# Reading compression windows straight from split keys with a stride, x's squares from a row-major copy, and other first pieces in a fused decoder layer

## The chip, the core and the metric

One core of a Trainium2 chip runs the whole layer in one launch. The metric is device microseconds from launch to end on that core, median of the runs shown. An execution's time is a little longer than the span of its profile, which goes from the first to the last instruction.

## What is computed

One decoder layer on 256 tokens of width 2048, all in float32: a token mixer (gMLP gating, dilated attention, native sparse attention), cross attention, and a squared-ReLU MLP of width 8192. What the change touches is the first normalization and the compressed keys and values:

```
def rms_norm(x, g):
    y = xf * lax.rsqrt(jnp.mean(xf * xf, axis=-1, keepdims=True) + EPS)
...
def compress_blocks(kraw, pos, w1, w2):      # blocks of 32 keys, stride 16 -> 15 blocks
    sub = kraw.reshape(bsz, ng, S // CMP_STRIDE, CMP_STRIDE, hd)
    blocks = jnp.concatenate([sub[:, :, :-1], sub[:, :, 1:]], axis=3) + pos
    h = jax.nn.gelu(blocks.reshape(bsz, ng, n_c, CMP_LEN * hd) @ w1)
    return h @ w2
```

`compress_blocks` runs for the keys and for the values, on 2 groups each; `w1` is 4096 x 128.

## The kernel before, in words

Every large product is made in a split form: a float32 operand is taken apart into a rounded part (`wh`, `hi`) and the remainder (`wl`, `lo`), and the product is hi·hi + hi·lo + lo·hi. ScalarE makes the rounded part by a copy (L82), VectorE the remainder by a subtraction (L83). A block of weights is 128 x 1024 numbers (512 KB). It is loaded by SyncE's queue into one of five `raw` buffers (`load_raw`, L78), split into one of three `wh` and three `wl` buffers, and used by TensorE.

`gemm_t` (L179) makes a transposed product: for each of the 4 blocks and each of 4 slices of 128 rows, `products_t` issues two matmuls with 512 moving columns (`mains`, L164: `wh` against the activation's hi and lo parts side by side) and two with 256 (`lows`, L169: `wl` against hi). `gemm` (L198) makes an untransposed product of 24 matmuls a block (L212). Matmuls here are named after their accumulator: `cmp`, `k`, `sg`, `wv`, `ph`, and so on.

The program begins with `cmp` (L240 to L265), the raw keys (m = 0) and values (m = 1) of the compressed branch. It loads x transposed (`xres`) and both weights in pieces, interleaved, in the steps `((1, 1, 2), (2, 2), (4,), (4,))` of 128-row slices for the four blocks b. Each piece of x is scaled and split into `hx` (`put_act`, L87 on ScalarE, L88 on VectorE), each piece of weights into `wh` and `wl`, and the products of a slice can start when its pieces are split. Then come `k0` (first keys of the other branches), `k1`, `sg` and `wv`. While `k0` runs, the generator `squares` adds up the squares of x: eight ScalarE squares (L101) and seven VectorE sums (L103) of 128 x 512, one sum on GpSimd (L115), two matmuls against a column of ones (`pss`, L117); from it come the reciprocal norm `rx` (L123) and its copy along the free dimension, `rxb` (two matmuls `psb`, L133).

While `k1` and `sg` run, the generator `compress` (L324) makes the compressed keys, then the values. VectorE gathers the 15 windows of 32 keys into `win` and adds the position (L330, which reads with a step of 16 numbers); the windows are split into `blk`, which lies as 32 slices of 60 columns (30 hi, 30 lo). For each of 32 positions l, two matmuls with 128 moving columns follow: `blk[:, l, :M2]` (30 stationary columns) with `wl` (L341), `blk[:, l, :]` (60) with `wh` (L343). They accumulate in `ph`; a copy `hh`, a product with a selection matrix `sel` (`pj`), a Gelu (`hg`, `hr`) and the second weight (`pk`, `pv`) end it. Gelu and the gates' Exp (L382) need different activation tables; a load of a table is an ACT instruction.

The order on each engine is set by a scheduler that works through the program with modelled costs; each engine and each queue then runs its list in order. Squares, `compress` and the gates so lie between the splits of weights on ScalarE and VectorE.

Of the kernel before, what the change touches and what calls it, by code (L numbers as in the profile page):

```python
# [37 lines left out]
def trunk_kernel(ctx: ExitStack, tc: tile.TileContext, a, out):  # L38
# [257 lines left out]
    rx = rstd(mean_eps(ssq, "mx"), "rx")
# [14 lines left out]
    for m in range(2):  # L311
# [9 lines left out]

    blk = slot("hC", "blk").rearrange("p k a s -> p (k a s)")[:, :LCMP * 2 * M2].rearrange("p (l m) -> p l m", l=LCMP)

    def compress():  # L324
        for m, which in enumerate(("k", "v")):
            win = cw[:, 4 * S:4 * S + LCMP * M2].rearrange("p (l g n) -> p l g n", l=LCMP, g=2)
# [426 lines left out]
def _masks(np):  # L753
# [4 lines left out]
    for window, d in ((128, 1), (512, 4), (2048, 16)):  # L758
        count += (dist >= 0) & (dist <= window) & (dist % d == 0)
    mb = np.where(count > 0, np.log(np.maximum(count, 1)), NEG).astype(np.float32)  # L760
    ends = np.arange(NCMP) * 16 + 31
# [20 lines left out]
def _arrays(np, i):  # L782
# [12 lines left out]
    def c1(w):  # L795
# [46 lines left out]
```

## Time and profile before

| | |
|---|---|
| median of 3 runs | 1195.46 us (1195.13 to 1196.47) |
| profiled execution | 1195.4 us |
| its span | 1193.6 us |
| TensorE matmuls busy | 1177.7 us, 99% |
| VectorE / ScalarE busy | 740.6 us / 589.2 us |
| chain that ended last | PE 97%, VectorE 1%, issue 1%, ScalarE 1% |
| DMA | 224 MB, mean 188 GB/s |

The table is read from the chain: where TensorE has 97% of it, only what makes TensorE wait or gives it more to do moves the end. "Busy" of a matmul includes a modelled end, so TensorE can be paced by something else for part of its busy time; starts of successive instructions tell more than durations. A load of stationary columns (PEld) runs beside the matmul before it.

### The profile page before, as it was taken

To read this page: it belongs to the slowest core of one execution; us is meant where nothing else is said; L and a number is where in the kernel's file an instruction comes from. 1 tells how busy PE (TensorE), PEld (TensorE's weight loads), DVE (VectorE), ACT (ScalarE), POOL (GpSimd) and SP (SyncE) were. 2 spreads that over 40 slices of the span, in tenths; PEclk is the share of its full clock that TensorE was granted. 3 is DMA by queue.
4 is the path that set the end of the run, shared out by engine and by line. 5 is a ranking of instruction groups with operands and counts; after the bars stand their busy time and mean duration, and the time that the engine had idled before them with its cause. 6 is when DMAs were issued, how large, how long until landed. Compare 5 with 4: busy or idle time off the path is not lost.

```text
span 1193.6 us, 16484 instructions
## 1 busy us (share of the span) xinstructions
PE 1177.7 (99%) x6450; PEld 1016.2 (85%) x6450; DVE 740.6 (62%) x939; ACT 589.2 (49%) x811; POOL 13.0 (1%) x18
## 2 busy tenths in 40 slices
PE   8999999999999999999999999999999999999996
PEld 6898888888888889888888888888888888888885
DVE  7875876569776567665545565545566445656554
ACT  7564555466544467544433444433444333444443
POOL 1000000000000000000000000000000000000000
PEclk9999999999999999999999999999999999999998
DMA  8776444556555554555555556665655655556653
GB/s 294 228 258 187 130 124 141 179 182 225 185 192 192 180 198 139 178 190 193 194 193 194 185 187 193 194 193 189 190 188 182 205 193 195 179 193 191 193 181 106
DMA packets 65673, 224.24 MB, mean 188 GB/s; under 512 B 7995, under 2 KB 9531, under 8 KB 65467
## 3 DMA queue, kind: packets, MB, share of 16 engines
q1 hardware_dynamic: 65307, 222.14, 57.9%
q8 instruction: 50, 0.82, 0.3%
q10 hardware_dynamic: 288, 1.05, 0.3%
q14 instruction: 28, 0.23, 0.1%
HBM read 221.06 MB, written 2.10 MB: 187 GB/s over the span
## 4 chain that ended last, share of the span: by engine, by line
PE 97%; DVE 1%; issue 1%; ACT 1%; DMA 0%; SPq 0%; POOLq 0%; POOL 0%; DVEq 0%; ACTq 0%
PE dn L212 28%; PE up L164 20%; PE up L169 10%; PE wo L164 5%; PE cq L164 3%; PE wo L169 2%; PE xo L153 2%; PE v L212 2%; PE bv L212 2%; PE mv L212 2%; PE k L164 1%; PE cq L169 1%; PE bq L164 1%; PE xq L164 1%; PE u L164 1%; PE mk L164 1%
## 5 line engine op out<-in xcount | busy, mean ns | idle before, releaser
L83 DVE TENSOR_TENSOR wl<-raw,wh 128x1024 fp32r<-128x1024 f32 (+3 forms) x412 | 493.2, 1200 | 325.7 <-ACT wh L82 324.6
L82 ACT ACTIVATE wh<-raw 128x1024 fp32r<-128x1024 f32 (+3 forms) x412 | 426.5, 1038 | 428.3 <-PE dn L212 185.5
L164 PE MATMUL up<-h,wh 128*128 128x512 f32 x1024 | 316.9, 395 | 0.0
L212 PE MATMUL dn<-wh,hid 128*128 128x512 f32 x992 | 306.1, 389 | 0.0
L169 PEld LDWEIGHTS up<-h,wl 128*128 128x128 f32 x1024 | 187.6, 188 | 42.2
L212 PEld LDWEIGHTS dn<-wh,hid 128*128 128x128 f32 x992 | 186.2, 188 | 38.7
L169 PE MATMUL up<-h,wl 128*128 128x256 f32 x1024 | 197.0, 279 | 0.0
L212 PE MATMUL dn<-wl,hid 128*128 128x512 f32 x496 | 193.2, 390 | 1.1 <-DVE wl L83 1.1
L164 PEld LDWEIGHTS up<-h,wh 128*128 128x128 f32 x1024 | 158.4, 189 | 2.7
L212 PEld LDWEIGHTS dn<-wl,hid 128*128 128x128 f32 x496 | 93.1, 188 | 21.4 <-DVE wl L83 2.0
L164 PE MATMUL wo<-mix,wh 128*128 128x512 f32 x256 | 79.1, 395 | 0.0
L169 PEld LDWEIGHTS wo<-mix,wl 128*128 128x128 f32 x256 | 46.5, 188 | 10.3
L193 ACT ACTIVATE half<-up 128x512 f32<-128x512 f32 x32 | 19.2, 599 | 63.6 <-PE up L164 63.6
L195 DVE TENSOR_TENSOR half<-up,half 128x512 f32<-128x512 f32 x32 | 22.2, 693 | 43.5 <-ACT half L193 43.5
L169 PE MATMUL wo<-mix,wl 128*128 128x256 f32 x256 | 49.0, 279 | 0.0
L164 PE MATMUL cq<-hx,wh 128*128 128x512 f32 x128 | 40.4, 396 | 0.0
L164 PEld LDWEIGHTS wo<-mix,wh 128*128 128x128 f32 x256 | 39.7, 189 | 0.8
L672 DVE SCALAR_TENSOR_TENSOR xt<-dn,m,xt 128x512 f32<-128x512 f32 (+1 forms) x34 | 22.9, 715 | 14.4 <-PE dn L212 14.4
L82 ACT ACTIVATE hid<-half 128x512 fp32r<-128x512 f32 x32 | 20.2, 632 | 16.6 <-DVE half L723 16.6
L169 PEld LDWEIGHTS cq<-hx,wl 128*128 128x128 f32 x128 | 23.5, 188 | 5.1
L164 PE MATMUL cmp<-hx,wh 128*128 128x512 f32 x64 | 21.3, 432 | 5.3 <-ACT wh L82 5.2
L169 PE MATMUL cq<-hx,wl 128*128 128x256 f32 x128 | 25.7, 280 | 0.0
(286 smaller groups left out, 1279.3 us busy)
## 6 DMA issues: line engine op xcount, KB each, us to landing
raw<-in_w_up SPq DMA_DIRECT2D x128, 512.0 KB, 4.4
raw<-in_w_down SPq DMA_DIRECT2D x128, 512.0 KB, 4.4
raw<-in_w_t SPq DMA_DIRECT2D x52, 512.0 KB, 3.8
raw<-in_w_out SPq DMA_DIRECT2D x32, 512.0 KB, 4.0
raw<-in_w_bv SPq DMA_DIRECT2D x8, 512.0 KB, 3.7
raw<-in_w_v SPq DMA_DIRECT2D x8, 512.0 KB, 3.6
raw<-in_w_mk SPq DMA_DIRECT2D x8, 512.0 KB, 4.1
raw<-in_w_q SPq DMA_DIRECT2D x8, 512.0 KB, 4.4
```

The lines of the kernel that those rows point to most:

```text
L82: nc.scalar.activation(hi, src, AF.Copy)
L83: nc.vector.tensor_tensor(lo, src, f32(hi), op=ALU.subtract)
L153: nc.tensor.matmul(acc[:, f, 0, :], w[:, kk, fs], x[:, kk, l, :], start=(kk == 0 and j == 0), stop=(kk == 3 and j == 2))
L164: nc.tensor.matmul(acc[:, f].rearrange("p a s -> p (a s)"), wh[:, kk, f * P:(f + 1) * P], xk, start=start, stop=stop)
L169: nc.tensor.matmul(acc[:, f, 0, :], wl[:, kk, f * P:(f + 1) * P], x[:, kk, 0, :], start=False, stop=False)
L193: nc.scalar.activation(lo, acc[:, :, 1, :], AF.Copy)
L195: nc.vector.tensor_tensor(d, acc[:, :, 0, :], lo, op=ALU.add)
L212: nc.tensor.matmul(acc[t][:, :n], lhs[k // 4][:, k % 4, l, ts], w[:, kk, :], start=(k == 0 and j == 0), stop=(k == KD - 1 and j == 2))
L672: nc.vector.scalar_tensor_tensor(xs, acc[t][:, cs], r3[:, t:t + 1], xs, op0=ALU.mult, op1=ALU.add)
```

## The change

It has four parts.

- **Windows.** `win` and `blk` are gone. The scaled keys are split as they lie, into `kps[m]` (hi and lo; for each, two groups of 256 positions and a third group that holds the 32 position vectors and zeros). The stationary operand for position l is a strided view: 96 columns, every 16th number from l on (48 for the `wl` product), 64 bytes apart. A group gives 16 columns: for the keys 15 windows and one that doesn't exist, for the positions one vector and zeros. `sel` (96 x 30) adds the position's row and drops the rest.
- **Squares of x.** x is loaded a second time with tokens on partitions (two loads of 1 MB), and four ScalarE squares of 128 x 1024 with an accumulated sum replace L101, L103, L115 and `pss`.
- **First pieces.** The steps become `((1, 3), (4,), (4,), (4,))`. The gains `gT` are loaded from ScalarE's queue.
- **First matmuls.** Eight float32 matmuls of 128 x 128 on a constant tile (`pw`) are issued ahead of all others.

The diff, cut:

```diff
+M3 = 3 * S // 16
...
+    nc.scalar.dma_start(gT, a["gT"])
...
+    wm = cp.tile([P, P], F32, name="wm")
+    nc.gpsimd.memset(wm, 1.0)
+    pw = pmisc.tile([P, P], F32, tag="sc", name="pw")
+    for _ in range(8):
+        nc.tensor.matmul(pw, wm, wm, start=True, stop=True)
...
-        for step in ((1, 1, 2), (2, 2), (4,), (4,))[b]:
+        for step in ((1, 3), (4,), (4,), (4,))[b]:
...
-                    if k == 0:
-                        nc.sync.dma_start(gT, a["gT"])
...
+    xs = [slot("hB", f"x{t}", F32).rearrange("p k a s -> p (k a s)") for t in range(2)]
+    for t in range(2):
+        with tc.issue_after(loads[-1].ins):
+            nc.sync.dma_start(xs[t], a["x"][t * P:(t + 1) * P, :])
...
+    kpf = [slot("hC", f"kp{m}").rearrange("p k a s -> p (k a s)")[:, :6 * S + 16] for m in range(2)]
+    kps = [t[:, :6 * S].rearrange("p (a g s) -> p a g s", a=2, g=3) for t in kpf]
...
-        for b in range(4):
-            for n in (2 * b, 2 * b + 1):
-                add_squares(ssq, xres[:, 2 * n:2 * n + 2, :], n == 0)
+        for t in range(2):
             yield
+            for i in range(2):
+                xi = xs[t][:, i * 1024:(i + 1) * 1024]
+                nc.scalar.activation(xi, xi, AF.Square, accum_out=ssqx[:, t, i:i + 1])
...
-    rx = rstd(mean_eps(ssq, "mx"), "rx")
+    nc.vector.tensor_reduce(mx, ssqx, axis=AX.X, op=ALU.add)
+    nc.vector.tensor_scalar(mx, mx, 1.0 / D, EPS, op0=ALU.mult, op1=ALU.add)
+    rx = rstd(mx, "rx")
...
+        split(kp[:, 0, :2, :], kp[:, 1, :2, :], km)
...
-            for g in range(2):
-                kr = kraw[:, 2 * m + g, :]
-                src = bass.AP(tensor=kr.tensor, offset=kr.offset, ap=[kr.ap[0], [1, LCMP], [16, NCMP]])
-                nc.vector.tensor_tensor(win[:, :, g, :], src,
-                                        C["posT"][:, :, None].to_broadcast([P, LCMP, NCMP]), op=ALU.add)
-            split(blk[:, :, :M2], blk[:, :, M2:], win.rearrange("p l g n -> p l (g n)"))
...
+                    blk = kpf[m][:, l:l + 16 * 2 * M3 - 15:16]
...
-                    nc.tensor.matmul(ph[:M2], blk[:, l, :M2], wl[:, i, :], start=False, stop=False)
+                    nc.tensor.matmul(ph[:M3], blk[:, :M3], wl[:, i, :], start=False, stop=False)
                     if l > 0:
-                        nc.tensor.matmul(ph, blk[:, l, :], wh[:, i, :], start=False, stop=(l == LCMP - 1))
+                        nc.tensor.matmul(ph, blk, wh[:, i, :], start=False, stop=(l == LCMP - 1))
```

How it moves the order. SyncE's queue at the program's start; the queue before (`xres` is x, `raw` the weights):

```order
L254 DMA xres<-in_xT 128x256
L257 DMA gT<-in_gT 128x64
L258 DMA raw<-in_w_t 128x256 x2
L254 DMA xres<-in_xT 128x256
L258 DMA raw<-in_w_t 128x256 x2
L254 DMA xres<-in_xT 128x512
L258 DMA raw<-in_w_t 128x512 x2
L254 DMA xres<-in_xT 128x512
L258 DMA raw<-in_w_t 128x512 x2
```

and with the change:

```order
L263 DMA xres<-in_xT 128x256
L265 DMA raw<-in_w_t 128x256 x2
L263 DMA xres<-in_xT 128x768
L265 DMA raw<-in_w_t 128x768 x2
L263 DMA xres<-in_xT 128x1024
L265 DMA raw<-in_w_t 128x1024 x2
L263 DMA xres<-in_xT 128x1024
L265 DMA raw<-in_w_t 128x1024
L263 DMA xres<-in_xT 128x1024
L265 DMA raw<-in_w_t 128x1024 x3
L286 DMA x_317<-in_x 128x2048
L286 DMA x_318<-in_x 128x2048
```

The second slice of x now comes with the third and fourth, and the two loads of x by rows stand behind the last `cmp` weights and the first weights of `k0`.

TensorE inside `compress`, a few of the 128 matmuls of `ph` (size: stationary by moving columns); before, with the buffers' numbers:

```order
L341 MATMUL ph_521<-wl_525,blk_493 30x128
L343 MATMUL ph_521<-wh_524,blk_493 60x128
```

and with the change:

```order
L354 MATMUL ph<-wl,kp_332 48x128
L356 MATMUL ph<-wh,kp_332 96x128
```

Their number and place stay; the stationary operand grows from 30 and 60 to 48 and 96 columns, and is now the strided view.

ScalarE between `sg` and `wv`, where the Gelu of the compressed values (`hr`) meets the Exp of the gates; before:

```order
L82 ACTIVATE wh<-raw 128x1024 x2
L365 ACTIVATE hr<-pj 128x15 x2
L381 ACTIVATE vs<-sg,rx 128x256
L382 ACT_TABLE_LOAD
L382 ACTIVATE gate<-sg,nrx 128x24
L381 ACTIVATE vs<-sg,rx 128x256
L382 ACTIVATE gate<-sg,nrx 128x24
L82 ACTIVATE wh<-raw 128x1024 x4
```

and with the change:

```order
L91 ACTIVATE wh<-raw 128x1024 x2
L398 ACTIVATE vs<-sg,rx 128x256
L399 ACT_TABLE_LOAD
L399 ACTIVATE gate<-sg,nrx 128x24
L398 ACTIVATE vs<-sg,rx 128x256
L378 ACT_TABLE_LOAD
L378 ACTIVATE hr<-pj 128x15 x2
L399 ACT_TABLE_LOAD
L399 ACTIVATE gate<-sg,nrx 128x24
L91 ACTIVATE wh<-raw 128x1024 x4
```

`hr` moves between the two gates, which takes two more loads of tables; on TensorE `pj`, from which `hr` is made, moves from the middle of the last blocks of `sg` to behind them. The `wh` behind it all are those of the third and fourth block of `wv` and of the two blocks after it.

## Rows read from the trace of the kernel before

**Rows 1.** The page: span, TensorE's busy time, shares of the chain that ended last.

```profile
span 1193.6 us, 16484 instructions
...
PE 1177.7 (99%) x6450; PEld 1016.2 (85%) x6450; DVE 740.6 (62%) x939; ACT 589.2 (49%) x811; POOL 13.0 (1%) x18
...
PE 97%; DVE 1%; issue 1%; ACT 1%; DMA 0%; SPq 0%; POOLq 0%; POOL 0%; DVEq 0%; ACTq 0%
```

**Rows 2.** Windows of the first 25 us: the stretch and its length, busy time of each engine (and instructions), granted clock, mean DMA share, GB/s.

```profile
0.00:5.00 5.00, 0.46 (x1) 0.47 (x2) 1.25 (x6) 2.78 (x5) 0.80 (x7) 1.00 0.48 142
5.00:10.00 5.00, 5.00 (x16) 3.95 (x15) 2.52 (x7) 3.18 (x8) 0.00 (x0) 1.00 0.91 260
10.00:15.00 5.00, 4.56 (x25) 3.84 (x25) 5.00 (x10) 5.00 (x11) 0.00 (x0) 1.00 1.00 369
15.00:20.00 5.00, 4.85 (x27) 3.79 (x26) 4.89 (x11) 5.00 (x10) 0.00 (x0) 1.00 1.03 414
20.00:25.00 5.00, 4.61 (x25) 3.69 (x25) 5.00 (x8) 4.78 (x9) 0.00 (x0) 1.00 1.03 345
```

**Rows 3.** Timeline of TensorE from the first matmul to the start of `k0`: start, time, line, product, shapes, count, idle time before it and its releaser.

```profile
4.54 2.07 PE L164 MATMUL cmp<-hx,wh 128*128 128x512 f32 x4 [4.54 <-ACT wh L82]
...
8.97 1.05 PE L169 MATMUL cmp<-hx,wl 128*128 128x256 f32 x4
10.46 1.25 PE L164 MATMUL cmp<-hx,wh 128*128 128x512 f32 x4 [0.44 <-ACT wh L82]
...
22.23 0.63 PE L164 MATMUL cmp<-hx,wh 128*128 128x512 f32 x2
...
22.92 0.63 PE L164 MATMUL cmp<-hx,wh 128*128 128x512 f32 x2
...
29.22 0.50 PE L117 MATMUL pss<-ones,ssq 128*128 128x1 f32 x4
29.58 0.48 PE L169 MATMUL cmp<-hx,wl 128*128 128x256 f32 x2
...
31.99 0.61 PE L164 MATMUL k<-hx,wh 128*128 128x512 f32 x2
```

**Rows 4.** Groups of instructions in the first 90 us, forms apart: line, engine, operation, out<-in, shapes, count; busy us, mean ns of one; idle time before them.

```profile
L83 DVE TENSOR_TENSOR wl<-raw,wh 128x1024 fp32r<-128x1024 f32 x26 | 31.5, 1223 | 8.0 <-ACT wh L82 7.9
L82 ACT ACTIVATE wh<-raw 128x1024 fp32r<-128x1024 f32 x27 | 28.1, 1056 | 12.1 <-PE k L164 4.8 <-PE wv L212 3.5 <-PE sg L212 1.6
...
L87 ACT ACTIVATE hx<-xres,gT 128x256 fp32r<-128x256 f32 x16 | 7.1, 498 | 2.9 <-DMA xres<-in_xT 2.0 <-DMA gT<-in_gT 0.9
...
L103 DVE TENSOR_TENSOR ssq<-ssq,sq 128x512 f32<-128x512 f32 x7 | 4.8, 688 | 0.1
L101 ACT ACTIVATE sq<-xres 128x512 f32<-128x512 f32 x7 | 4.1, 616 | 0.0
...
L382 ACT ACT_TABLE_LOAD x1 | 1.3, 1283 | 0.0
```

**Rows 5.** The instructions of `ph` (shortest, median and longest ns, first and last start), and of `psc`, a later product with 128 stationary and 30 moving columns.

```profile
L341 PEld LDWEIGHTS ph<-wl,blk x64: 105/107/112, 46.4 to 73.1; 128*30 128x30 f32 x64
...
L343 PEld LDWEIGHTS ph<-wh,blk x62: 130/132/135, 46.5 to 73.2; 128*60 128x60 f32 x62
...
L447 PEld LDWEIGHTS psc<-kcT,q x32: 187/192/192, 105.7 to 152.4; 128*128 128x128 f32 x32
```

**Rows 6.** Timeline of TensorE: successive matmuls of `ph`, and 16 of `psc`.

```profile
47.08 0.22 PE L341 MATMUL ph<-wl,blk 128*30 128x128 f32 x1
47.14 0.22 PE L343 MATMUL ph<-wh,blk 128*60 128x128 f32 x1
47.20 0.22 PE L341 MATMUL ph<-wl,blk 128*30 128x128 f32 x1
...
150.73 1.94 PE L447 MATMUL psc<-kcT,q 128*128 128x30 f32 x16
```

**Rows 7.** VectorE's readers of the raw keys (the gather with a step of 16 numbers, the scaling without one), and a later operation on rows of 15 numbers that lie together.

```profile
L330 DVE TENSOR_TENSOR cw<-cw,posT x4: 996/1003/1010, 38.2 to 44.3; 128x480 f32<-128x480 f32 x4
...
L313 DVE TENSOR_TENSOR cw<-cw,rxb x2: 683/684/686, 37.0 to 37.6; 128x512 f32<-128x512 f32 x2
...
L459 DVE TENSOR_TENSOR scm<-scm,cm x2: 284/284/284, 123.6 to 155.1; 128x120 f32<-128x120 f32 x2
```

**Rows 8.** Timeline of ScalarE, VectorE and TensorE between `sg` and `wv`, each engine by itself.

```profile
77.08 0.48 ACT L381 ACTIVATE vs<-sg,rx 128x256 f32<-128x256 f32 x1 [0.61 <-PE sg L212]
77.56 1.28 ACT L382 ACT_TABLE_LOAD   x1
78.86 0.28 ACT L382 ACTIVATE gate<-sg,nrx 128x24 f32<-128x24 f32 x1
79.04 0.47 ACT L381 ACTIVATE vs<-sg,rx 128x256 f32<-128x256 f32 x1
...
79.56 2.02 ACT L82 ACTIVATE wh<-raw 128x1024 fp32r<-128x1024 f32 x2
...
80.65 1.23 DVE L83 TENSOR_TENSOR wl<-raw,wh 128x1024 fp32r<-128x1024 f32 x1
...
76.82 0.28 PE L212 MATMUL wv<-wh,hx 128*128 128x256 f32 x1
76.94 0.28 PE L212 MATMUL wv<-wl,hx 128*128 128x256 f32 x1
```

More of the change, by code (lines that the diff above doesn't have):

```diff
@@ L273, in consts @@
                 nc.sync.dma_start(C[name], a[name].partition_broadcast(P) if name == "bs" else a[name])
-    consts([("ident", [P, P]), ("posT", [P, LCMP]), ("sel", [2 * M2, M2]), ("hmask", [P, 4]), ("rowv", [P, 2])])
+    xs = [slot("hB", f"x{t}", F32).rearrange("p k a s -> p (k a s)") for t in range(2)]
+    for t in range(2):
+        with tc.issue_after(loads[-1].ins):
+            nc.sync.dma_start(xs[t], a["x"][t * P:(t + 1) * P, :])
+    consts([("ident", [P, P]), ("posT", [P, LCMP]), ("sel", [2 * M3, M2]), ("hmask", [P, 4]), ("rowv", [P, 2])])
     ident = C["ident"]
-    cw = slot("hC", "cw", F32).rearrange("p k a s -> p (k a s)")
-    kraw = cw[:, :4 * S].rearrange("p (g s) -> p g s", g=4)
+    kraw = slot("hB", "kraw", F32).rearrange("p k a s -> p (k a) s")
+    kpf = [slot("hC", f"kp{m}").rearrange("p k a s -> p (k a s)")[:, :6 * S + 16] for m in range(2)]
+    kps = [t[:, :6 * S].rearrange("p (a g s) -> p a g s", a=2, g=3) for t in kpf]
     vs = slot("hC", "vs", F32).rearrange("p k a s -> p (k a s)")
@@ L283, in trunk_kernel @@
     kcat = slot("hB", "kcat").rearrange("p (g a) b s -> p g a b s", g=2)
-    ssq = sp.tile([P, 2, S], F32, tag="ssq", name="ssq")
+    ssqx = cp.tile([P, 2, 2], F32, name="ssqx")
     def squares():
@@ L289, in squares @@
             join(acc, "cmp", kraw[:, 2 * m:2 * m + 2, :])
-        for b in range(4):
-            for n in (2 * b, 2 * b + 1):
-                add_squares(ssq, xres[:, 2 * n:2 * n + 2, :], n == 0)
+        for t in range(2):
             yield
+            for i in range(2):
+                xi = xs[t][:, i * 1024:(i + 1) * 1024]
+                nc.scalar.activation(xi, xi, AF.Square, accum_out=ssqx[:, t, i:i + 1])
+        yield
     acc_k0 = gemm_t(hx, a["w_t"][KV], "k0", between=squares())
-    rx = rstd(mean_eps(ssq, "mx"), "rx")
+    mx = cp.tile([P, 2], F32, name="mx")
+    nc.vector.tensor_reduce(mx, ssqx, axis=AX.X, op=ALU.add)
+    nc.vector.tensor_scalar(mx, mx, 1.0 / D, EPS, op0=ALU.mult, op1=ALU.add)
+    rx = rstd(mx, "rx")
     rxb = along_free(rx, "rxb")
@@ L309, in join_split @@
         split(hi, lo, j)
-    for m in range(2):
+    for m, kp in enumerate(kps):
         km = kraw[:, 2 * m:2 * m + 2, :]
         nc.vector.tensor_tensor(km, km, rxb[:, None, :].to_broadcast([P, 2, S]), op=ALU.mult)
+        split(kp[:, 0, :2, :], kp[:, 1, :2, :], km)
     join_split(acc_k0, kcat[:, :, 0, 0, :], kcat[:, :, 1, 0, :], "k0", rxb)
@@ L320, in trunk_kernel @@
     vcz = cp.tile([P, 2, 4, HD], F32, name="vcz")
-    blk = slot("hC", "blk").rearrange("p k a s -> p (k a s)")[:, :LCMP * 2 * M2].rearrange("p (l m) -> p l m", l=LCMP)
     def compress():
         for m, which in enumerate(("k", "v")):
-            win = cw[:, 4 * S:4 * S + LCMP * M2].rearrange("p (l g n) -> p l g n", l=LCMP, g=2)
-            for g in range(2):
-                kr = kraw[:, 2 * m + g, :]
-                src = bass.AP(tensor=kr.tensor, offset=kr.offset, ap=[kr.ap[0], [1, LCMP], [16, NCMP]])
-                nc.vector.tensor_tensor(win[:, :, g, :], src,
-                                        C["posT"][:, :, None].to_broadcast([P, LCMP, NCMP]), op=ALU.add)
-            split(blk[:, :, :M2], blk[:, :, M2:], win.rearrange("p l g n -> p l (g n)"))
-            ph = pmisc.tile([2 * M2, P], F32, tag="sc", name="ph")
+            ph = pmisc.tile([2 * M3, P], F32, tag="sc", name="ph")
             for b in range(4):
@@ L338, in compress @@
                     l = 8 * b + i
+                    blk = kpf[m][:, l:l + 16 * 2 * M3 - 15:16]
                     if l == 0:
-                        nc.tensor.matmul(ph, blk[:, l, :], wh[:, i, :], start=True, stop=False)
-                    nc.tensor.matmul(ph[:M2], blk[:, l, :M2], wl[:, i, :], start=False, stop=False)
+                        nc.tensor.matmul(ph, blk, wh[:, i, :], start=True, stop=False)
+                    nc.tensor.matmul(ph[:M3], blk[:, :M3], wl[:, i, :], start=False, stop=False)
                     if l > 0:
-                        nc.tensor.matmul(ph, blk[:, l, :], wh[:, i, :], start=False, stop=(l == LCMP - 1))
+                        nc.tensor.matmul(ph, blk, wh[:, i, :], start=False, stop=(l == LCMP - 1))
                 yield
@@ L347, in compress @@
                 nc.sync.dma_start(w2, a[f"c{which}2"])
-            hh = sp.tile([2 * M2, P], F32, tag="hh", bufs=1, name="hh")
+            hh = sp.tile([2 * M3, P], F32, tag="hh", bufs=1, name="hh")
             nc.scalar.activation(hh, ph, AF.Copy)
@@ L371, in compress @@
             yield
+    for kf, kp in zip(kpf, kps):
+        nc.gpsimd.memset(f32(kp[:, 0, 2, LCMP:]), 0.0)
+        nc.gpsimd.memset(f32(kf[:, 5 * S + LCMP:]), 0.0)
+        split(kp[:, 0, 2, :LCMP], kp[:, 1, 2, :LCMP], C["posT"])
     cgen = compress()
@@ L760, in _masks @@
     mb = np.where(count > 0, np.log(np.maximum(count, 1)), NEG).astype(np.float32)
+    sel = np.zeros((3, 16, 2, NCMP), np.float32)
+    for g in range(2):
+        sel[g, :NCMP, g] = np.eye(NCMP)
+    sel[2, 0] = 1
     ends = np.arange(NCMP) * 16 + 31
@@ L770, in _masks @@
         "triu": np.triu(np.ones((P, P), np.float32)),
-        "sel": np.concatenate([np.eye(M2), np.eye(M2)]).astype(np.float32),
+        "sel": np.tile(sel.reshape(M3, M2), (2, 1)),
         "hmask": np.repeat(np.eye(4), 32, axis=0).astype(np.float32),
@@ L802, in _arrays @@
     d = {
-        "xT": actT(f["x"][0]), "memT": actT(f["mem"][0]),
+        "x": f["x"][0], "xT": actT(f["x"][0]), "memT": actT(f["mem"][0]),
         "gT": np.stack([gains(f[n][0]) for n in ("norm_mix", "norm_xattn", "norm_mem", "norm_mlp")], axis=1),
```

## The prediction, written before the change ran

> **What bounds the kernel now.** I read the chain of waits first: TensorE has 97% of it, and its matmuls are busy for 1177.7 of 1193.6 us [rows 1]. So a term counts only where TensorE waits or gets more to do; freed ScalarE and VectorE time counts nothing by itself. Then the windows and the timeline of the head, the stretch where TensorE does wait. The 32 groups of `cmp`, each two matmuls of 512 and two of 256 columns, take 0.69 us each when nothing holds them (22.23 to 22.92) [rows 3]: 22.1 us in all. They begin at 4.54 and `k0` begins at 31.99 [rows 3], 27.45 us; 5.3 us are lost. The first four groups account for 2.7 of it: they fill 4.54 to 10.02 (8.97 + 1.05), 5.48 us instead of 2.76 [rows 3]. Four matmuls of 256 columns in 1.05 us, less the tail of the last, start some 213 ns apart, which is the 1.2 GHz level of the clock; at 22.23 they run at 2.4 GHz. (The granted clock reads 1.00 there [rows 2], against the rows; I go by the starts.) `pss` takes 0.36 (29.22 to 29.58) [rows 3]. The rest, some 2 us, is waiting for splits, at 10.02 to 10.46 and where blocks of 1024 columns first arrive. From 10 to 25 us ScalarE and VectorE have no free time, and the DMA engines neither [rows 2]. Behind `k0` TensorE has no gap that a faster neighbour could close.
>
> **Head.** The squares leave ScalarE's and VectorE's queues of the head: 8 x 0.616 = 4.9 us and 7 x 0.688 = 4.8 us [rows 4]. What then ends last is the transfers. By the windows 0.71 MB have come by 5 us, 2.01 by 10, 3.86 by 15, 5.93 by 20 [rows 2]. Block 0 is now the first slices (0.39 MB), then x (0.39), weights (0.39), weights (0.39): 1.57 MB, in by 5 + 0.86/0.260 = 8.3 us. A copy of 768 columns takes some 0.85 us (between 0.616 for 512 and 1.056 for 1024 [rows 4]), so the second `wh` stands at 9.15. TensorE's list wants it after one pair of matmuls; the rest of block 0 (six groups, 4.15 us, less that pair's 0.45) ends at 12.9. Block 1: x in at 10.25, four copies of 0.44 (0.498 with pipeline ends [rows 4]) to 12.0, `wh` to 13.05, `wl` to 14.25: the first low products wait 0.8 us, and block 1 ends near 19.5. Blocks 2 and 3 are then paced by TensorE: 16 x 0.69 = 11.0, `k0` at 30.5, a gain of 1.5. Where larger pieces let the transfers run from 4 us at the 414 GB/s that the stretch from 15 us has [rows 2], weights of block 0 stand 1.7 us earlier, the wait in block 1 shrinks, and the gain is 3.8. These are the ends; I take **-2.0**, nearer the first, since the measured rate of that stretch is the nearer row. In it the missing `pss` is 0.36. The eight `pw` matmuls start near 1.1 us, when TensorE could do nothing else until 4.1; two passes each at up to 213 ns make 3.4 us, to 4.5: they take no time from `cmp`. If TensorE leaves 1.2 GHz as long after its first work as before (10.02 - 4.54), it is at 6.6 us instead of 10; slices two to four then run fast, but they start at 9.15 anyway, so this is worth little beyond the 1.5.
>
> **Second load of x.** 2.1 MB behind 6.3 + 0.5 MB: 8.9 MB are in by 20 + 2.97/0.414 = 27.2 us [rows 2]. Two squares of 1024 (as the copy, 1.056 [rows 4]) end at 29.4, sums, power and diagonal near 32; `psb` stands behind the first matmuls of `k0`'s second block, 30 + 2.8 + 0.45 = 33.2. Covered by 1 us; without that cover, each us of delay is one of TensorE. The split of the scaled keys, 2 x 0.68 and two copies, ends some 6 us before the first `ph`. Both at nothing. `gT`, now on ScalarE's queue, frees SyncE 0.4 us earlier; the first matmul waits for `pw`.
>
> **Compressed products.** 128 matmuls with 128 moving columns, now 60 ns apart: a pair takes 0.12 us (47.08 to 47.20) [rows 6]. The load of 30, 60 and 128 contiguous stationary columns takes 107, 132 and 192 ns [rows 5]; where matmuls are short, loads of 128 set the pace, (1.94 - 0.26)/15 = 0.112 us each [rows 6], 0.875 ns a column. So 60 columns (0.053) hide under a matmul today. 96 contiguous columns would be 0.084, 48 still hidden: a pair of 0.144, and 64 pairs cost 64 x 0.024 = 1.5 us. That is the lower end; less is excluded, since neither the number of matmuls nor their columns fall.
>
> But the columns now lie 64 bytes apart, and no load in the trace reads so. The nearest row is VectorE's gather, with the same step over the same keys: 480 numbers in 1003 ns, where 512 contiguous take 684 [rows 7]. At 1.05 ns a number (1223 for 1024 against 684 for 512 [rows 4, 7]) 480 would take 650; the step adds 353/480 = 0.74 ns to each. That it is the step and not the short runs of 15 follows from the 120 numbers in runs of 15 in 284 ns [rows 7], no more than the contiguous price. With 0.74 added a column of a load costs 1.61 ns: 96 take 0.155, 48 take 0.077, neither hidden, a pair 0.232, and the term is 64 x 0.112 = 7.2 us. At the gather's full 1.79 ns a number it is 0.172 + 0.086, 8.8 us: the upper end. I take **+7.2**.
>
> The Trainium skill's page "SBUF — State Buffer", in the section "Specifications (TRN2)", says that memory lines are 16 bytes long and that full bandwidth needs at least two hits on a line, every crossing being penalised. The gather agrees, with 1.79 ns against 1.05; the page gives no price, and no run here shows one for a stationary load.
>
> **Tables.** Two more loads of 1.283 us [rows 4] stand between `sg` and the third block of `wv`. From the end of `sg`, on the clock of [rows 8] with `pj` moved behind it: `vs` at 76.75, table, gate, `vs` to 79.15, table to 80.43, two `hr` to 80.67, table to 81.95, gate, and the third `wh` to 83.2 instead of 80.6. VectorE does `hr`'s copy by 81.0, after the gate three small operations, then the third `wl` at 83.25 to 84.45. TensorE starts `wv` at 76.82 and does 24 matmuls of 0.12 us a block [rows 8]; it reaches `pv` after seven of block 2, at 80.5, and waits 0.4 for `hr`; 0.36 later it goes on, and reaches the second matmul of the third block at 83.5, where `wl` is 0.95 late. **+1.35**; ends 0 (the chain ahead starts earlier by what ScalarE has been freed of) and 2.6 (both loads).
>
> Removed work of `win` and `blk`, four gathers and two splits, lay beside TensorE and is worth nothing. GpSimd's memsets are done before anyone waits.
>
> **Sum.** The profiled execution took 1195.4 us (0.06 under the median). -2.0 + 7.2 + 1.35 = +6.55: **1202.0 us**. By its parts' ends, 1199 to 1204.5. A measurement of this kernel can tell about 0.2%, 2.4 us, from no change.
>
> **Rivals.**
> A. *The strided load costs no more than a contiguous one.* Loads and matmuls read through different paths than VectorE, and a load runs at half a matmul's column rate, so it may have room. Then -2.0 + 1.5 + 1.35 = +0.85: 1196.3, no change (1195 to 1198). For it: a load is slow already (0.875 ns, where a moving column takes 0.69/1536 = 0.45 [rows 3]). Against it: the gather. The Trainium skill's page "TensorE: Matmul & The Clock Gate", section "LDWEIGHTS", makes a load's time the number of its columns over 1.2 GHz and nothing else; by that rule the sum is this rival's, and the contiguous rows agree (0.875 ns against 0.83).
>
> B. *The head gives all that it can, and the loads stay hidden: faster.* Block 0's last weights land by 6.6 instead of 8.3, for -3.8; a strided pair costs 0 to 24 ns more; and `wv` waits for nothing, because ScalarE reaches the tables earlier. Mean -3.0: 1192.4. It decides from a pair of `ph` at 0.14 us or less and `k0` before 28.5. For it: 4 KB rows run at 414 GB/s later on. Against it: the DMA engines are 91% busy at 260 GB/s between 5 and 10 us [rows 2], so it was not a lack of requests.
>
> C. *The new first matmuls do not bring the faster clock sooner.* Then block 0's slices run at 1.2 GHz to 10 us, and some 0.6 us of the head's gain is lost; this moves each case up, within its range.
>
> **How the numbers follow.** Forecast 0.50, A 0.28, B 0.22. The forecast gives slower; A mostly same, a little slower (its upper end is over 2.4); B faster, a little same. Faster 0.21, same 0.27, slower 0.52. Cases of both signs hold most of the chance, so the forecast's own range is 1199 to 1204.5; the range over all, 1192.5 to 1204.5, leaves out the lower half of B and what lies above the strided upper end.
>
> **What would show it.** Right: loads of 96 columns well over 160 ns and of 48 over 122 (the contiguous line through 107, 132, 192), pairs of `ph` near 0.23 us, each eight of them nearly 1 us longer; `k0` near 30 us; a wait of TensorE for `wl` in `wv`'s third block of some 1 us and for `pv` of 0.4. Wrong: pairs at 0.14 or less. If `psb` shows a wait, the second load of x was late; if matmuls after 7 us still start 427 ns apart at 512 columns, `pw` did nothing.

## The result, and the profile after

The change makes the kernel slower: 1205.82 us, median of 6 runs (1204.78 to 1206.18), against 1196.36 us (1195.13 to 1196.99, 6 runs) beside it. The ratio is 1.0079, 95% interval 1.0069 to 1.0090: 9.5 us. The forecast of 1202.0 had the sign and the largest term, but not the head of the program, and the time lies above its range.

The page of the profile after, to be read against [rows 1] ("..." marks lines left out, here and below):

```profile
span 1203.0 us, 16480 instructions
...
PE 1186.6 (99%) x6462; PEld 1025.7 (85%) x6462; DVE 732.6 (61%) x927; ACT 591.6 (49%) x811; POOL 11.4 (1%) x22
```

The span grew by 9.4 us and TensorE's busy time by 8.9, while VectorE got 8 us freer and ScalarE stayed level: work moved onto the engine that sets the end. The first windows, with the columns of [rows 2] and to be read against them:

```profile
0.00:5.00 5.00, 4.01 (x19) 3.72 (x19) 1.17 (x6) 2.72 (x5) 1.41 (x10) 1.00 0.55 151
5.00:10.00 5.00, 2.45 (x11) 1.64 (x11) 3.17 (x6) 3.12 (x6) 0.00 (x0) 1.00 1.00 372
10.00:15.00 5.00, 5.00 (x30) 4.21 (x29) 4.54 (x8) 4.89 (x10) 0.00 (x0) 1.00 1.02 419
```

From 5 to 10 us the DMA engines bring 372 GB/s instead of 260, yet TensorE is busy for 2.45 of the 5 us: the large second piece comes as one lump, and TensorE waits for it. TensorE's timeline of the head, then `ph` (to be read against [rows 3] and [rows 6]):

```profile
0.99 3.63 PE L70 MATMUL pw<-wm 128*128 128x128 f32 x16 [0.99 <-POOL wm L67]
4.38 1.30 PE L173 MATMUL cmp<-hx,wh 128*128 128x512 f32 x4
5.51 0.64 PE L178 MATMUL cmp<-hx,wl 128*128 128x256 f32 x4
8.33 0.73 PE L173 MATMUL cmp<-hx,wh 128*128 128x512 f32 x2 [2.18 <-ACT wh L91]
9.44 0.73 PE L173 MATMUL cmp<-hx,wh 128*128 128x512 f32 x2 [0.37 <-ACT wh L91]
...
29.71 0.63 PE L173 MATMUL cmp<-hx,wh 128*128 128x512 f32 x2
31.36 0.74 PE L173 MATMUL k<-hx,wh 128*128 128x512 f32 x2 [1.02 <-ACT wh L91]
32.62 0.50 PE L178 MATMUL k<-hx,wl 128*128 128x256 f32 x2 [0.53 <-DVE wl L92]
...
35.51 0.60 PE L142 MATMUL psb<-dg,ones 128*128 128x128 f32 x4
...
46.63 0.27 PE L353 MATMUL ph<-wh,kp 128*96 128x128 f32 x1
...
51.92 0.22 PE L354 MATMUL ph<-wl,kp 128*48 128x128 f32 x1
...
53.91 0.46 PE L178 MATMUL k<-hx,wl 128*128 128x256 f32 x2
```

Two things are to be seen. First, `cmp` is done some 1.8 us earlier than before: its last group starts at 29.71, and `k0` follows 0.46 later where nothing holds it. But `k0` starts at 31.36, after a wait for ScalarE, and waits once more for VectorE; `ph` starts at 46.63 against 46.35 before, so the head has given nothing. Second, 16 matmuls of `ph` take 1.99 us (51.92 to 53.91), 0.249 a pair, where they took 0.12 a pair [rows 6].

ScalarE's timeline shows what `k0` waited for (first, the second copy of weights of `cmp`'s block 0):

```profile
8.54 0.84 ACT L91 ACTIVATE wh<-raw 128x768 fp32r<-128x768 f32 x1 [0.26 <-DMA raw<-in_w_t]
...
21.75 1.06 ACT L91 ACTIVATE wh<-raw 128x1024 fp32r<-128x1024 f32 x1 [1.72 <-PE cmp L173]
23.31 1.06 ACT L308 ACTIVATE x<-x 128x1024 f32<-128x1024 f32 x1 [0.50 <-DMA x<-in_x]
...
27.57 0.60 ACT L202 ACTIVATE half<-cmp 128x512 f32<-128x512 f32 x1 [2.06 <-PE cmp L173]
28.06 1.05 ACT L308 ACTIVATE x<-x 128x1024 f32<-128x1024 f32 x1
...
30.14 0.21 ACT L91 ACTIVATE kp<-posT 128x32 fp32r<-128x32 f32 x1
30.26 1.04 ACT L91 ACTIVATE wh<-raw 128x1024 fp32r<-128x1024 f32 x1
```

The copy of weights at 21.75 is the last of `cmp`; `k0`'s first is the one at 30.26, behind both squares of x's second half (from 28.06). Between `sg` and `wv`, ScalarE and then TensorE (to be read against [rows 8]):

```profile
87.25 1.28 ACT L378 ACT_TABLE_LOAD   x1
88.55 0.26 ACT L378 ACTIVATE hr<-pj 128x15 f32<-128x15 f32 x2
88.82 1.28 ACT L399 ACT_TABLE_LOAD   x1
90.12 0.28 ACT L399 ACTIVATE gate<-sg,nrx 128x24 f32<-128x24 f32 x1
90.30 2.94 ACT L91 ACTIVATE wh<-raw 128x1024 fp32r<-128x1024 f32 x3
...
88.25 0.40 PE L221 MATMUL wv<-wh,hx 128*128 128x256 f32 x2
89.01 0.71 PE L381 MATMUL pv<-w2v,hr 128*128 128x128 f32 x4 [0.36 <-DVE hr L379]
...
91.47 0.40 PE L221 MATMUL wv<-wh,hx 128*128 128x256 f32 x2
92.66 0.39 PE L221 MATMUL wv<-wl,hx 128*128 128x256 f32 x1 [0.79 <-DVE wl L92]
```

Behind the tables TensorE waits 0.36 us at `pv` and 0.79 us in `wv`'s third block.

### The profile page after: what moved, and what is told of

Its sections match the earlier page's. It is cut to its first block, busy times and chain, and to the rows that moved or that the text cites. A ratio compares the mean times of both kernels' runs of the same rounds, so it can differ in the third digit from the quotient of the medians.

```text
span 1203.0 us, 16480 instructions
## 1 busy us (share of the span) xinstructions
PE 1186.6 (99%) x6462; PEld 1025.7 (85%) x6462; DVE 732.6 (61%) x927; ACT 591.6 (49%) x811; POOL 11.4 (1%) x22
## 4 chain that ended last, share of the span: by engine, by line
PE 95%; ACT 1%; DVE 1%; issue 1%; DMA 1%; SPq 0%; POOLq 0%; POOL 0%; ACTq 0%; DVEq 0%
PE dn L221 27%; PE up L173 20%; PE up L178 10%; PE wo L173 5%; PE cq L173 2%; PE wo L178 2%; PE xo L162 2%; PE v L221 2%; PE bv L221 2%; PE mv L221 2%; PE cq L178 1%; PE xq L173 1%; PE mk L173 1%; PE u L173 1%; PE bq L173 1%; PE bk L173 1%
## 5 line engine op out<-in xcount | busy, mean ns | idle before, releaser
L92 DVE TENSOR_TENSOR wl<-raw,wh 128x1024 fp32r<-128x1024 f32 (+2 forms) x408 | 493.1, 1210 | 336.0 <-ACT wh L91 334.4
L91 ACT ACTIVATE wh<-raw 128x1024 fp32r<-128x1024 f32 (+2 forms) x408 | 426.1, 1046 | 435.9 <-PE dn L221 185.5
L162 PE MATMUL xo<-oT,wh 128*128 128x256 f32 x128 | 23.9, 287 | 0.0
```

What stands on the lines that cost most here:

```text
L91: nc.scalar.activation(hi, src, AF.Copy)
L92: nc.vector.tensor_tensor(lo, src, f32(hi), op=ALU.subtract)
L162: nc.tensor.matmul(acc[:, f, 0, :], w[:, kk, fs], x[:, kk, l, :], start=(kk == 0 and j == 0), stop=(kk == 3 and j == 2))
```

## Experiments

The runs were taken in groups. Times of different groups are compared by their ratio to the kernel before, which ran beside each group (1195.7 to 1196.0 us); behind a ratio stands its 95% interval. Diffs are cut ("...").

**1. The step between columns.** The whole view of the keys kept at 96 and 48 columns, but not where they belong: the columns are taken next to each other (`step1`), 8 bytes apart (`step2`) or 16 bytes apart (`step4`), so the selection of windows is left out.

```diff
...
-                    blk = kpf[m][:, l:l + 16 * 2 * M3 - 15:16]
+                    blk = kpf[m][:, l:l + 1 * (2 * M3 - 1) + 1:1]
```

> The changed kernel with 96 and 48 stationary columns as before, but lying together (numbers l to l+95 of the split keys, so the windows are not the right ones: the selection of windows is left out; instructions, their order and sizes stay). Theory 1, the 64-byte step makes the stationary load slow: a load of 96 hides all but 0.084 us, a pair of ph takes 0.14 to 0.15 us instead of 0.2525, and the time falls by 64 x 0.105 = 6.5 to 7 us against the changed kernel, to about 1199 (ratio to the kernel before near 1.002). Rival, the larger number of columns does it: the pair stays near 0.25 us and the time near 1205.8.

> The changed kernel with the stationary columns taken 8 bytes apart (every second number; again not the right windows). Two numbers then come from each 16 bytes. Theory 1a, a price per 16-byte line with two numbers enough to hide it: as with columns that lie together, a pair of ph at 0.14 to 0.15 us. Theory 1b, any step costs: a pair between 0.16 and 0.25 us.

> The changed kernel with the stationary columns 16 bytes apart (every fourth number; not the right windows). Theory 1a: each column is on a 16-byte line of its own, so it is as slow as 64 bytes, a pair of ph at 0.25 us. Theory 1b, the price grows with the step: a pair clearly under 0.25, near 0.18 to 0.22 us.

`step1` took 1199.37 us, ratio 1.0027 (1.0017 to 1.0037), by the ratios some 6 us less than the change; `step2` (a single run) 1199.84, `step4` (a single run) 1206.75. The loads of `ph` in the change, in `step1`, in `step2` and in `step4` (shortest, median and longest ns), to be read against [rows 5]:

```profile
L354 PEld LDWEIGHTS ph<-wl,kp x64: 159/179/185, 46.7 to 81.2; 128*48 128x48 f32 x64
...
L356 PEld LDWEIGHTS ph<-wh,kp x62: 241/261/266, 46.8 to 81.3; 128*96 128x96 f32 x62
```

```profile
L354 PEld LDWEIGHTS ph<-wl,kp x64: 121/125/125, 46.7 to 74.7; 128*48 128x48 f32 x64
...
L356 PEld LDWEIGHTS ph<-wh,kp x62: 160/162/166, 46.8 to 74.8; 128*96 128x96 f32 x62
```

```profile
L354 PEld LDWEIGHTS ph<-wl,kp x64: 121/125/131, 48.1 to 76.5; 128*48 128x48 f32 x64
...
L356 PEld LDWEIGHTS ph<-wh,kp x62: 164/168/174, 48.2 to 76.5; 128*96 128x96 f32 x62
```

```profile
L354 PEld LDWEIGHTS ph<-wl,kp x64: 163/186/190, 47.8 to 83.2; 128*48 128x48 f32 x64
...
L356 PEld LDWEIGHTS ph<-wh,kp x62: 251/274/279, 48.0 to 83.3; 128*96 128x96 f32 x62
```

The second 48 columns cost (162 - 125)/48 = 0.77 ns each when they lie together, (168 - 125)/48 = 0.90 at 8 bytes, (274 - 186)/48 = 1.83 at 16 and (261 - 179)/48 = 1.71 at 64. So it is mostly the step that costs. Nearly all of its price comes between 8 and 16 bytes, as theory 1a had it, and a longer step adds nothing more.

**2. Everything but the windows.** `oldwin` has `win`, `blk` and `sel` as before, and with them the old place of `hr` (one table load); head and squares are the change's.

```diff
...
-                    blk = kpf[m][:, l:l + 16 * 2 * M3 - 15:16]
...
-                    nc.tensor.matmul(ph[:M3], blk[:, :M3], wl[:, i, :], start=False, stop=False)
+                    nc.tensor.matmul(ph[:M2], blk[:, l, :M2], wl[:, i, :], start=False, stop=False)
```

> The changed kernel with the compressed branch of the kernel before (win, blk, 30 and 60 columns that lie together); second load of x, first pieces, pw and gT's queue stay as changed. The order of ScalarE there becomes the one of before, with hr ahead of the gates and one table load instead of three. If the three terms read from the changed trace add up (products +8.2, tables and hr +1.5, head about 0): 1205.8 - 9.7 = 1196.1, the same as the kernel before within 1 us, ratio 0.998 to 1.001. If the new head is worth its 2 us after all: 1194.3, ratio 0.998.

1196.52 us (10 runs), ratio 1.0004 (0.9995 to 1.0013). Products and tables together are the whole loss, within the interval; the head as it stands is worth nothing that can be measured.

**3. ScalarE's order.** `sqlate` issues all four squares behind the latest copy of weights, `sqmid` only those of x's second half behind `k0`'s first copy. `oldwin_sq` and `oldwin_sqmid` do the same on `oldwin`.

```diff
...
-                nc.scalar.activation(xi, xi, AF.Square, accum_out=ssqx[:, t, i:i + 1])
+                with tc.issue_after(splits[-1].ins):
+                    nc.scalar.activation(xi, xi, AF.Square, accum_out=ssqx[:, t, i:i + 1])
```

> The changed kernel with ScalarE's squares of x issued behind the latest copy of a weights' half instead of where the loop stands, so that k0's first copy of weights comes ahead of them. Theory 1 (k0 waits for ScalarE's order and for nothing else): k0 starts near 30.2 us instead of 31.36, its first low products by 31.5 instead of 32.62, nothing waits later, and the time is 1.5 to 2.0 us under the changed kernel's, near 1204. Theory 2 (the squares are needed soon enough that a later place gives the time back): the matmul that spreads the power of x's mean square, psb, shows a wait of about 1 to 2 us, and the time stays within 0.5 us of the changed kernel's 1205.8.

> Windows and contiguous split columns as in the kernel before, one table load as there, the rest of the change as it is (first pieces, pw, second load of x), and x's squares issued behind k0's first copy of weights. Theory 1 (the head's gain of some 2 us was lost only to ScalarE's order): k0 starts near 30.2 us and the time is 1.5 to 2.0 us under the same kernel with the squares in the loop's place (1196.5), so 1194.5 to 1195, a ratio to the kernel before of 0.9985 to 0.9995. Theory 2 (what k0 no longer waits for it waits for elsewhere: the low half from VectorE, the power of x): the ratio stays at 1.000 to 1.001.

> The changed kernel with only the squares of x's second half moved on ScalarE, behind k0's first copy of weights; those of the first half stay where they fill ScalarE's wait for cmp. The power of x is then due some 2 us later than in the changed kernel and not 6, as in the run before with all squares moved. Theory 1 (the head's gain was lost to ScalarE's order, and the run before lost half of it again because the scaled keys came late): k0 starts near 30.2 us without a wait, no wait near 48 us, and the time is 1.5 to 2.0 us under the changed kernel's, 1203.8 to 1204.3. Theory 2 (each us that k0 starts earlier comes back as a wait in what hangs on the power of x): k0 starts early and a wait of 1 us or more stands between 36 and 50 us; the time stays within 0.7 us of 1205.8.

> Windows and contiguous split columns as in the kernel before and one table load, the rest of the change as it is, and only the squares of x's second half behind k0's first copy of weights. Theory 1: k0 starts near 30.2 us, the windows' chain on VectorE is 2 us later than before instead of 6 and holds nothing up; 1.5 to 2.0 us under the same kernel with the squares in their place (1196.5), so near 1194.7, a ratio of 0.998 to 0.9995 to the kernel before. Theory 2: the windows' additions, which stand on VectorE ahead of low halves of weights, come late enough to hold TensorE up near 50 us, as in the run with all squares moved (2.1 us there); the ratio is 1.000 to 1.002.

| | time, us | ratio to before | `cmp`'s last group, `k0` | new waits of TensorE |
|---|---|---|---|---|
| `sqlate` | 1205.38 | 1.0078 (1.0065 to 1.0092) | 29.45, 29.91 | 0.96 at 48.38, keys `kp` |
| `sqmid` | 1203.89 | 1.0067 (1.0051 to 1.0082) | 32.02, 32.49 | 0.53 at 36.59, `wl` |
| `oldwin_sq` | 1200.57 | 1.0039 (1.0026 to 1.0052) | 32.06, 32.52 | 0.96 at 50.97, 2.11 at 53.82 |
| `oldwin_sqmid` | 1196.62 | 1.0008 (0.9999 to 1.0017) | 31.45, 31.91 | 0.53 at 36.01, 0.74 at 49.63 |

In all four `k0` starts 0.46 us behind `cmp`'s last group: the wait for `wh` was ScalarE's order, as theory 1 has it. But waits come up later, as theory 2 has it, if in other places than it named (`psb` waits in none): 0.53 to 3.07 us together, where the change had 1.02 and 0.53 at `k0`. TensorE's rows in `sqlate`, then in `oldwin_sq`:

```profile
29.91 0.62 PE L174 MATMUL k<-hx,wh 128*128 128x512 f32 x2
...
48.38 0.74 PE L174 MATMUL k<-hx,wh 128*128 128x512 f32 x2 [0.96 <-DVE kp L93]
```

```profile
50.97 0.74 PE L174 MATMUL k<-hx,wh 128*128 128x512 f32 x2 [0.96 <-ACT wh L92]
53.82 0.50 PE L179 MATMUL k<-hx,wl 128*128 128x256 f32 x2 [2.11 <-DVE wl L93]
```

The squares must be done before `rxb`, `rxb` before the keys and the windows, and these stand on ScalarE and VectorE ahead of weights of `k1`. Only `sqmid` came out lower by what theory 1 asked (1203.89), and its interval and `sqlate`'s overlap with the change's. `oldwin_sq` lost some 4 us against `oldwin`, which neither of its theories had. What the profiles add, one for each version: from `cmp`'s last group to the end of the span the change takes 1173.3 us, `sqlate` 1172.4 and `sqmid` 1172.2; `oldwin` takes 1163.7, `oldwin_sqmid` 1163.7 and `oldwin_sq` 1167.6. By that count the new order gives back some 1 us of the 1.5 in the change, and nothing with the old windows.

**4. The gates behind `hr`** (two table loads fewer).

```diff
...
-        nc.scalar.activation(gate[:, t].rearrange("p h c -> p (h c)"), acc[t][:, S:NG], AF.Exp, scale=nrx[:, t:t + 1])
+        with tc.issue_after(gelus[-1].ins):
+            nc.scalar.activation(gate[:, t].rearrange("p h c -> p (h c)"), acc[t][:, S:NG], AF.Exp, scale=nrx[:, t:t + 1])
```

> The changed kernel with the two Exp of the gates issued behind hr's Gelu, so that one table load of 1.28 us and not three lies between sg and wv's third block. Theory (the tables cost about 1.4 us): the waits of 0.36 us at pv and 0.79 us in the third block of wv are gone and the time is 1.2 to 1.8 us under the changed kernel's, near 1204.4. Rival (those waits are covered by something later, or the gates then come too late for their readers): the time stays within 0.4 us of 1205.8.

1204.32 us, 1.0066 (1.0051 to 1.0082), an interval that overlaps with the change's; the trace is clearer. TensorE waits neither at `pv` nor in `wv`, and from `cmp`'s last group to the end of the span it takes 1202.6 - 31.02 = 1171.6 us against 1203.0 - 29.71 = 1173.3 in the change: 1.7 us less.

**5. Pieces and first matmuls.** `nopw` is the change without `pw`; `oldwin_112` is `oldwin_sqmid` with block 0 in pieces of 1, 1 and 2 slices; `b_head` is the kernel before with `pw`, the new pieces and `gT` on ScalarE's queue, but with its own squares.

```diff
...
-        for step in ((1, 3), (4,), (4,), (4,))[b]:
+        for step in ((1, 1, 2), (4,), (4,), (4,))[b]:
```

> The changed kernel without the eight matmuls of pw. Theory (they bring the faster clock sooner, but the feed sets the pace of the first block): the first two slices of cmp start some 427 ns apart at 512 columns, then TensorE waits for the second copy of weights all the same; k0 waits for ScalarE at the same place, and the time is 0 to 0.6 us above the changed kernel's. Rival 1: all slices up to about 10 us run at 1.2 GHz and the time is 1.5 to 2.5 us above. Rival 2: pw only kept TensorE busy and the time is the same or a little less.

> The kernel of the run beside it with block 0's first pieces as in the kernel before (one, one and two slices) instead of one and three; blocks 1 to 3 whole. Theory 1 (TensorE waits 2.2 us near 8.3 us because the second piece is too large to be there sooner): that wait splits into smaller ones of 1.2 us together at most, and the time is 0.8 to 1.5 us less. Theory 2 (bytes set the pace, not the pieces: 0.39 MB of x and 0.79 MB of weights are in at the same time either way): the waits' sum stays at 1.8 to 2.5 us and the time within 0.4 us.

> The kernel before with the change's first pieces, pw and gT on ScalarE's queue alone; x's squares stay on ScalarE and VectorE in the head, from the split copies' source, and there is no second load. Theory 1 (the squares on those two queues paced the head): cmp's blocks 0 and 1 still wait for splits 2 us and more in all, k0 starts at 30.5 to 32, and the time is 0 to 1.5 us under the kernel before. Theory 2 (the pieces and the clock did it, not the squares): k0 starts near 30 and the time is 1.5 to 2.5 us under it. By either, a later place of the windows on VectorE could take it back.

`nopw`: 1205.61 us, 1.0081 (1.0068 to 1.0095), the change's time; its first four matmuls of 512 columns take 2.04 us against 1.30, the next four (from 8.48) 2.28, so they run at the slower level as its rival 1 had it (the granted clock reads 1.00 there, as in [rows 2]), and `cmp`'s last group starts at 30.64. Yet the time is the same. `oldwin_112`: 1196.44, 1.0006 (0.9998 to 1.0015); three waits for `wh` (0.56, 1.04 and 0.70 us) take the place of one, as its theory 2 said. `b_head`: 1201.30, 1.0044 (1.0031 to 1.0057), which neither theory had: `cmp`'s last group starts at 33.90, and the scaling of the keys and the gathers of the windows (49 to 53 us on VectorE) stand ahead of weights of `k1`, which waits 0.97 and 1.88 us. The granted clock is at 0.50 from 10 to 16 us in its profile, so a part of the loss is the clock's (experiment 6); how much was not taken apart. The new pieces without the new squares lose 5 us: the two parts of the head belong together.

**6. The clock in the wait.** `fill` and `oldwin_fill` put ten more matmuls of `pw` behind the first slice of `cmp`; `after_again` is the change once more.

```diff
...
-                lows()
+                low = lows()
+                if kk == 0 and fill:
+                    with tc.issue_after(low.ins):
+                        for _ in range(fill):
+                            nc.tensor.matmul(pw, wm, wm, start=True, stop=True)
```

> The changed kernel with ten more matmuls of pw behind the first slice of cmp, 20 passes of some 0.11 us, 2.3 us in all, where TensorE waits 0.9 to 3.5 us for the second piece. Theory 1 (idleness in that wait makes the clock fall in some executions): the granted clock stays at 1.00 from 10 to 14 us, cmp's last group starts near 29.7, and the time is 0.5 to 1.5 us under that of the unchanged program beside it. Theory 2 (what varies is when the piece arrives, and the clock has no share): cmp ends as late as in the others, the time is the same or up to 1 us more, where the ten last longer than the wait.

> The kernel with the old windows and the changed head (1196.5 us in an earlier run, spans of 1193.4 to 1195.4 in two groups) with the same ten matmuls. Theory 1: the upper group is gone, spans of 1193.3 to 1194 and a time near 1195.5, a ratio to the kernel before of 0.999 to 1.000. Theory 2: the ratio stays at 1.000 to 1.001 with both groups.

> The changed kernel once more. Theory 1: the executions fall into two groups some 1 to 1.5 us apart, the upper with the lower mean clock, and most lie in the upper, since 1203.0 was the shortest span of six; the profile may be of either. Theory 2: one group about 1204 us, with no link between span and clock.

`fill` 1205.54 us, 1.0087 (1.0073 to 1.0100); `after_again` 1205.64, 1.0093 (1.0078 to 1.0107), spans from 1202.8 (mean clock 0.999) to 1207.7 (0.994); `oldwin_fill` 1195.78, 1.0003 (0.9994 to 1.0012). In the five executions of `after_again` the longer the span, the lower the mean clock, as theory 1 had it, though they spread over 4.9 us and not in two groups. Windows of `after_again`, columns as above, and TensorE's rows beside them:

```profile
10.00:12.00 2.00, 2.00 (x10) 1.70 (x9) 1.99 (x5) 1.96 (x5) 0.00 (x0) 0.67 1.02 418
12.00:14.00 2.00, 2.00 (x8) 1.81 (x7) 1.54 (x3) 1.94 (x3) 0.00 (x0) 0.50 1.03 422
...
34.00:38.00 4.00, 3.77 (x13) 3.20 (x14) 3.57 (x8) 1.29 (x2) 0.00 (x0) 0.57 0.51 157
```

```profile
8.73 0.73 PE L173 MATMUL cmp<-hx,wh 128*128 128x512 f32 x2 [1.98 <-ACT wh L91]
9.63 0.74 PE L173 MATMUL cmp<-hx,wh 128*128 128x512 f32 x2 [0.17 <-ACT wh L91]
...
11.54 1.05 PE L173 MATMUL cmp<-hx,wh 128*128 128x512 f32 x2
...
31.30 0.63 PE L173 MATMUL cmp<-hx,wh 128*128 128x512 f32 x2
32.97 0.73 PE L173 MATMUL k<-hx,wh 128*128 128x512 f32 x2 [1.04 <-ACT wh L91]
...
49.81 0.27 PE L353 MATMUL ph<-wh,kp 128*96 128x128 f32 x1
```

The same program that ran at full clock in its first profile (29.71) falls to 1.2 GHz here behind the wait for the second piece, and again behind the wait at `k0`; `cmp` ends 1.6 us later, `ph` starts 3.2 later, and the span is 3.1 longer. With the filler the clock stays up (`fill`):

```profile
10.00:12.00 2.00, 2.00 (x14) 1.78 (x14) 1.88 (x5) 2.00 (x5) 0.00 (x0) 1.00 1.03 420
12.00:14.00 2.00, 2.00 (x13) 1.51 (x12) 1.64 (x2) 1.88 (x4) 0.00 (x0) 1.00 1.04 424
```

Of the 12 profiled executions with `pw`, the new pieces and no filler, 8 show a granted clock near half between 8 and 14 us, 4 do not. Leaving out `b_head`, `cmp`'s last group starts at 30.8 to 32.1 in the former and at 29.4 to 29.8 in the latter; the length of the wait doesn't part them (it fell after 1.30 us in `gate`, and stayed after 2.18 in the change). Both profiles with filler have it at 1.00 and the group at 29.5; two profiles against four of twelve do not settle that the filler did it.

The waits ahead of the fall add up to about the same in the two profiles of the change (2.18 and 0.37 us; 0.49, 1.98 and 0.17). Of the 1.6 us at `cmp`'s end 0.2 stand before the fall (9.63 against 9.44), and the fall is worth the other 1.4; the second fall costs another 1.6 up to `ph`. By these single profiles `pw` gains 0.9 us on `nopw` at `cmp`'s end where the clock stays up (29.71 against 30.64) and loses 0.7 where it falls (31.30). The change's profiled execution is the shortest of its six; the other five have lower mean clocks (0.996 to 0.997 against 0.998), so the same fall may be in them, which no profile shows.

What the filler saves in the median (0.1 us in `fill` against `after_again`, 0.7 in `oldwin_fill` against `oldwin`) is within the intervals and stays open; theory 1 had asked for 0.5 to 1.5 us in `fill`. No version beats the kernel before: the best, `oldwin_fill`, is level with it.

## Why the prediction came out as it did

| step | forecast, us | profile, us | by which rows |
|---|---|---|---|
| head | -2.0 | +0.28 | `ph` starts at 46.63 against 46.35 |
| products | +7.2 | +7.60 | from there to the start of `wv`: 38.07 against 30.47 |
| tables | +1.35 | +1.76 | from there to the eviction of `wv`: 13.90 against 12.14 |
| sum | +6.55 | +9.4 | span; 0.24 comes back later |

The rows that bound the stretches, before (the start of `wv` stands in [rows 8]) and after (the first of `ph` is shown above):

```profile
46.35 0.22 PE L340 MATMUL ph<-wh,blk 128*60 128x128 f32 x1
88.96 0.84 ACT L393 ACTIVATE vs<-wv,rx 128x256 f32<-128x256 f32 x2 [1.82 <-PE wv L212]
```

```profile
84.70 0.36 PE L221 MATMUL wv<-wh,hx 128*128 128x256 f32 x1
98.60 0.84 ACT L410 ACTIVATE vs<-wv,rx 128x256 f32<-128x256 f32 x2 [1.82 <-PE wv L221]
```

**The head failed**, by 2.3 us of the 2.9. "k0 at 30.5, a gain of 1.5" was right for `cmp`: it could have been 30.17. The step that failed is "Second load of x": "Covered by 1 us". It asked when the squares would be done (29.4 forecast, 30.2 in the trace) and who waits for their result (`psb`, which at 35.51 waits for nothing, as forecast). It did not ask what stands behind them in ScalarE's list. That is `k0`'s first copy of weights: 1.02 us there, 0.53 for the remainder that VectorE takes from it, and slower first matmuls behind both. The prediction places that copy nowhere. Experiment 3 shows the wait gone with the order, and also that the gain is not to be had by that alone. The transfers, which the step "Head" named as what would end last, came as forecast (the second copy of weights of block 0 ends at 9.38, forecast 9.15).

**Products.** The mechanism was right and taken from the right row. A strided column costs 1.71 ns; I had 1.61 from adding the gather's 0.74 to a contiguous load, while the gather's full price of 1.79, the upper end, is nearer. Sixteen matmuls take 1.03 us more than before, 8.2 us over eight blocks; about 0.6 of that is offset within the stretch, where by the starts of TensorE's rows `pj` takes 0.4 us less and `sg` 0.3 less. Rival A is refuted: `step1` has its price, a pair near 0.145 us, with the columns lying together, `step2` nearly so at 8 bytes, and the change, at 64 bytes, has not.

Two places of the Trainium skill bear on this. The Trainium skill's page "SBUF — State Buffer", section "Specifications (TRN2)", asks for at least two hits on a 16-byte line: by that rule two columns to a line should be nearly free and one to a line dear, and the loads agree (168 and 274 ns for 96 columns). The Trainium skill's page "TensorE: Matmul & The Clock Gate", section "LDWEIGHTS (loading the stationary operand)", has the number of columns over 1.2 GHz and no step: near the measurement for each further column where they lie together (0.77 ns against 0.83), wrong by a factor of two for those 16 or 64 bytes apart, where the measurement decides.

**Tables.** Both waits came where forecast and in size (0.36 and 0.79 against 0.4 and 0.95). By the starts they cost more, since idle time leaves out the modelled end of the matmul before: from 88.25 to 89.01 and from 91.47 to 92.66 two matmuls take 0.76 and 1.19 us instead of 0.24, a delay of 0.52 and 0.95. The other 0.3 of 1.76 is at first matmuls that start further apart than the 0.12 of those behind them. `gate` gives it back.

**Rivals B and C.** B is refuted on both counts: the loads of `ph` show, and `k0` begins at 31.36, not before 28.5. C is refuted for the first slice: its rows run at the fast level (1.30 us for four matmuls of 512 columns, 2.07 before [rows 3]) from 4.38 us on, earlier than the 6.6 us that the prediction allowed. What no case had is that the faster clock may be lost again in the wait that the larger pieces make.

**The range** was put together wrongly. 1199 to 1204.5 is called "its parts' ends", but the upper ends, -1.5, +8.8 and +2.6, add up to +9.9, which is 1205.3. As a difference to the kernel before, the measured 9.5 us lies inside that sum; it lies outside of the stated range. And the head's ends were -1.5 and -3.8: it had no end at zero, though "no gain, because something else is late next" was the one thing its rows couldn't exclude.

## What to carry to other kernels

A float32 stationary operand may be read with a step of up to two numbers at little cost (0.90 ns a column against 0.77); with one column to 16 bytes a column costs about twice as much (1.83), which showed here because matmuls of 128 columns, 0.06 us apart where nothing holds them [rows 6], are too short to hide the loads. Before a piece of work on a side engine is called covered, look at what stands behind it in that engine's list, not only at who reads its result. Larger first pieces raised the transfer rate (372 GB/s against 260 from 5 to 10 us) but made one long wait, and a wait early on can cost more than its length: the clock fell behind it in 8 of 12 profiles, at 1.4 us where two profiles of one program could be compared.

## What was not expected of the hardware

- The price of a step comes nearly all at once: 96 columns load in 162 ns together, 168 at 8 bytes, 274 at 16 and 261 at 64.
- An accumulated square is followed by an instruction of its own, ACTIVATION_READ_ACCUMULATOR, 0.18 to 0.19 us on ScalarE; four of them stand in the head.
- The granted clock after a wait of about 2 us differs between executions of one program: 1.00 in one and 0.50 in the other, 1.6 us apart at `cmp`'s end, 1.4 of it behind the fall.
